# Attention-value products of two heads: float32 by turns on the two halves of the output columns, in place of three products of split halves on all columns

## The chip, the cores and the metric

The kernel runs on one core of a Trainium2 chip. Its metric is the device time of one execution in microseconds (us). The engines are TensorE (PE; its weight loads are listed as PEld), VectorE (DVE), ScalarE (ACT), GpSimd (POOL) and SyncE (SP, which issues the weight DMAs). PE products go to PSUM and are read from there by DVE or ACT.

## The reference

One sequence of 256 positions by 1024 features runs through three blocks: a layer of gated softmax attention with forget gates ("fox") and one of compressed, selected and windowed attention ("nsa"); a layer of stick-breaking and dilated attention with a feed-forward network; a layer of pooling and block attention with a mixture of experts. Every attention ends in the same kind of product: probabilities times values, per head of 64 columns.

```
p = jax.nn.softmax(logits, axis=-1).astype(v.dtype)          # fox, nsa, dilated, block attention
w = jnp.where(mask, jnp.exp(log_sigmoid(z) + after), 0.0)    # stick-breaking
o = jnp.einsum('bhqk,bkhd->bqhd', p, v)                      # the product that the change concerns
```

There are 16 heads in fox, 16 in nsa (each with two such products, selected and windowed, on top of a small one with compressed keys), 16 in the second block's mixer (8 stick-breaking, 8 dilated) and 8 in the third's. All is float32.

## The kernel before

Activations lie transposed, features on the 128 partitions, 256 positions along the free side. Weights come as pieces of 128x1024 by DMA. ACT rounds each piece to a high part (`whi`, line 241) and DVE makes the low part (`wlo`, line 242); a projection is three products per 128x128 tile (lines 450 to 452: high by high, low by high, high by low), in the type float32r. These projections are most of PE's instructions.

In each mixer a generator for the attention is woven between the steps of the projections (`weave`, with a rate for each mixer). What the generators record is not yet the order on an engine: a scheduler places each engine's instructions by when it reckons their operands to be ready, so an attention product can be parted by products of the projections. Per head the attention makes scores (lines 545, 546, 555 or 961, 962), a softmax, three transpositions on PE into a PSUM tile `t`, a copy of it into SBUF, and the product with the values. Keys are in two blocks of 128, and the first 128 queries see only the first, so the probabilities of a head are 384 columns: 256 for key block 0, 128 for key block 1.

The last two steps are done in two ways:

- fox and the second block's mixer ("mixer2"): ACT writes the rounded probabilities into `pth` (line 610) and DVE the rest into `ptl` (line 611), for a pair of heads side by side; the values are split likewise when they leave PSUM, `vh` by ACT (line 601) and `vl` by DVE (line 602). `pair_av` (line 628) then takes the values of both heads, 128 columns wide, as the weights, and streams both heads' probabilities: three products of 512 columns for key block 0 and three of 256 for key block 1. Half of what it writes is one head's probabilities by the other head's values, and is not read: `gated_pair` and `finish` take the two right quarters, in two instructions each (lines 646 and 1123).
- nsa and the third block's mixer ("mixer3"): `attn_transpose` copies the transposed probabilities in float32 to `ptw` (line 588, three buffers), and `attn_av` (lines 595 and 596) does one head at a time in float32, its 64 value columns as the weights, into the half of the output tile `o` that belongs to the head. Each float32 product appears in the trace as two weight loads and two matmuls. In nsa the four products of a chunk (two heads, two branches) follow one product of all 128 columns with 32 rows (`VCB`, line 1013).

Of the kernel before, what the change touches and what calls it, by code (L numbers as in the profile page):

```python
# [9 lines left out]
F32 = mybir.dt.float32  # L10
# [5 lines left out]
OP = mybir.AluOpType  # L16
# [254 lines left out]
def program(tc, A, out, upto=99):  # L271
    nc = tc.nc
    ctx = ExitStack()
    with ctx:
# [323 lines left out]
        def values(dst, c, p, r):  # L598
# [5 lines left out]
        def probs(pt, h, src):  # L604


            if h % 2 == 0:
                pt[h // 2] = [ph.tile([P, 2, 384], F32R, name=n, bufs=2) for n in ("pth", "ptl")]
# [4 lines left out]
        def transposed(pn):  # L613
            p = ps.tile([P, 384], F32, name="t")
            for i in range(3):
                nc.tensor.transpose(p[:, i * P:i * P + P], pn[:, i * P:i * P + P], ident)
            return p

        def pair_av(pt, v, c):


            o = ps.tile([P, 2, S], F32, name="o")
            hi, lo = pt
            for kb in range(2):
                q = slice(0, S) if kb == 0 else slice(S, S + P)
                vh, vl = (t[:, kb, c] for t in v)
                for i, (w, x) in enumerate(((vh, hi), (vl, hi), (vh, lo))):
                    nc.tensor.matmul(o[:, :, kb * P:], w, x[:, :, q], start=kb == 0 and i == 0, stop=kb == 1 and i == 2)
            return o

# [7 lines left out]
        def gated(og, c, po, sz):  # L638
            t = wk.tile([P, S], F32, name="sp")
            nc.vector.tensor_tensor(t, po, sz[:, c, :], op=OP.mult)  # L640
            split(og, c, t)

        def gated_pair(og, c, o, sz):
            t = wk.tile([P, S], F32, name="sp")
            for e, a in enumerate(HALF):
                nc.vector.tensor_tensor(t[a], o[a, e, :], sz[a, c, :], op=OP.mult)
            split(og, c, t)
# [32 lines left out]
        def fox(st1):  # L680
# [50 lines left out]

            vN = [ph.tile([P, 2, D], F32R, name=n) for n in ("vh", "vl")]
# [16 lines left out]
            def fox_attn():  # L749
                st, pt = {}, {}  # L750
# [35 lines left out]
        def nsa(st1):  # L786
# [159 lines left out]
            def attn():  # L946
# [48 lines left out]

                def trans(c):
                    for e in range(2):
                        for b in range(2):
                            stage[c, e, b] = attn_transpose(stage[c, e, b], CP[b])
                            yield  # L1000
                    p = ps.tile([32, 256], F32, name="t")
                    c2 = stage[c, "c"]
# [4 lines left out]
                    stage[c, "c"] = t  # L1007
                    yield

                def av(c):  # L1010
                    gp = c // 4
                    o = ps.tile([P, S], F32, name="o")
                    nc.tensor.matmul(o, VCB[:, gp, :], stage[c, "c"], start=True, stop=False)
                    for e in range(2):
                        oh = o[e * 64:e * 64 + 64, :]
                        g = 2 * gp + e
                        for b in range(2):
                            attn_av(oh, stage[c, e, b], lambda kb: vN[:, kb, b * 256 + g * 64:b * 256 + g * 64 + 64], False, b == 1)
                            yield
                    while cnt["z"] <= c:  # L1020
                        yield
                    gated(og, c, o, sz)
                    yield

                for i in range(9):
                    if i:
                        while len(done) < 2:
                            yield
                        yield from comp(i - 1)
                    if i < 8:  # L1030
                        while cnt.get("nq", 0) <= i:
                            yield
                        yield from scores(i)
                    if i:
                        yield from trans(i - 1)
                        yield from av(i - 1)

# [47 lines left out]
        def mixer2(st1):  # L1085
# [18 lines left out]

            vN = [ph.tile([P, 2, D], F32R, name=n) for n in ("vh", "vl")]

            def v_evac(c, tb, p):
                values(vN, (tb, slice(c * 512, c * 512 + 512)), p, rc[:, tb:tb + 1])

# [10 lines left out]
            def finish(c, po):  # L1120
                o = ph.tile([P, S], F32, name="fo", bufs=2)
                for e, a in enumerate(HALF):
                    nc.scalar.copy(o[a], po[a, e, :])
                sq = wk.tile([P, S], F32, name="sq")
                nc.scalar.activation(sq, o, AF.Square)
                p = ps.tile([P, S], F32, name="t")
# [8 lines left out]
            def attn():  # L1135
                st, pt = {}, {}

                for i in range(19):
# [24 lines left out]
                    if 1 <= i <= 16:  # L1163
                        h = i - 1
                        if h < 8:
                            z, sp = st[h]
                            nc.tensor.matmul(z[:, 0:384], C["ntri"], sp, start=False, stop=False, skip_group_check=True)
                            nc.tensor.matmul(z[:, 128:256], neg, sp[:, 256:384], start=False, stop=True, skip_group_check=True)
                            w = wk.tile([P, 384], F32, name="ptw")
                            nc.scalar.activation(w, z[:, 0:384], AF.Exp)  # L1170
                            probs(pt, h, w)
                        else:
                            probs(pt, h, transposed(st[h]))
                        yield
                    if i >= 3 and i % 2 == 1 and i <= 17:
                        c = (i - 3) // 2
                        finish(c, pair_av(pt.pop(c), vN, slice(c * P, c * P + P)))
                        yield
# [73 lines left out]
        def mixer3(st1):  # L1252
# [58 lines left out]
            def attn():  # L1311
                st, po = {}, {}
                for i in range(11):
# [11 lines left out]
                    if 2 <= i <= 9:  # L1325
                        h = i - 2
                        c = h // 2
                        if h % 2 == 0:
                            po[c] = ps.tile([P, S], F32, name="o")
                        attn_av(po[c][(h % 2) * 64:(h % 2) * 64 + 64, :], st[h], lambda kb: vN[:, kb, h * 64:h * 64 + 64])  # L1330
                        if h % 2 == 1:
                            nc.scalar.copy(oa[0][:, c, :], po[c])
                            nc.vector.tensor_tensor(oa[1][:, c, :], po[c], oa[0][:, c, :].bitcast(F32), op=OP.subtract)
                        yield
# [412 lines left out]
```

## Time and profile before

| | us |
|---|---|
| median of three runs | 1717.55 (1711.0 to 1719.35) |
| the profiled execution | 1714.88 |
| its span, first to last instruction | 1713.1 |
| PE busy | 1658.1 (97%) |
| PE weight loads busy | 1532.3 (89%) |
| DVE busy | 1304.1 (76%) |
| ACT busy | 976.3 (57%) |

A matmul's length in the trace is from its start to its modelled end, and the next one starts before that: what one costs the engine is read from start to start. The stages of the four mixers lie at about 28 to 160 us (fox), 200 to 345 (nsa, whose attention starts near 230), 360 to 490 (mixer2) and 720 to 800 (mixer3's attention). The mean granted TensorE clock is 0.994.

### The profile page before, as it was taken

How to read it: one execution, taken by the hardware profiler on the slowest of the kernel's cores; microseconds unless marked ns; L12 is line 12 of the kernel's file. 1: busy time of each engine (PE TensorE's matmuls, PEld its weight loads, DVE VectorE, ACT ScalarE, POOL GpSimd, SP SyncE). 2: the span in 40 equal slices, each digit the busy share in tenths (PEclk: the TensorE clock that was granted, in tenths of full speed). 3: DMA queues.
4: the chain of work that ended last, by engine and by line, in shares of the span. 5: the costliest groups of instructions: out<-in, count | busy, mean ns of one | idle time of the engine just before them, and what ended most of it. 6: DMA issues, size and time to landing. Idle time of an engine off the chain costs nothing.

```text
span 1713.1 us, 31723 instructions
## 1 busy us (share of the span) xinstructions
PE 1658.1 (97%) x12052; PEld 1532.3 (89%) x12052; DVE 1304.1 (76%) x2715; ACT 976.3 (57%) x1853; POOL 189.4 (11%) x198
## 2 busy tenths in 40 slices
PE   9999999989899999999999999999999999999997
PEld 7999888778789999889999999999999988888886
DVE  6887878699867766786768988888999566666665
ACT  5775567558855555566544455554444555555554
POOL 2000244340130000111046000000000000000000
PEclk9999999999999999999999999999999999999999
DMA  7444542387437877435555555454454556555663
GB/s 252 136 136 150 169 166 64 105 268 243 149 111 259 267 262 245 143 118 173 175 172 161 161 164 157 159 161 156 155 161 159 174 195 196 190 193 195 196 189 120
DMA packets 84088, 300.07 MB, mean 175 GB/s; under 512 B 10144, under 2 KB 11040, under 8 KB 83680
## 3 DMA queue, kind: packets, MB, share of 16 engines
q1 hardware_dynamic: 83360, 296.39, 53.5%
q8 instruction: 94, 1.54, 0.4%
q10 hardware_dynamic: 576, 1.66, 0.3%
q14 instruction: 58, 0.48, 0.1%
HBM read 296.04 MB, written 1.05 MB: 173 GB/s over the span
## 4 chain that ended last, share of the span: by engine, by line
PE 52%; DVE 3%; ACT 0%; issue 0%; POOLq 0%; POOL 0%; DVEq 0%; ACTq 0%
PE s L1624 10%; PE t L1624 10%; PE pj L450 5%; PE pj L451 5%; PE pj L452 5%; PE o L1584 3%; PE s L450 2%; PE t L450 2%; PE s L452 2%; PE s L451 2%; PE t L451 2%; PE t L452 2%; DVE wlo L242 1%; PE s L1433 0%; PE o L595 0%
## 5 line engine op out<-in xcount | busy, mean ns | idle before, releaser
L241 ACT CAST whi<-wraw 128x1024 fp32r<-128x1024 f32 x504 | 528.9, 1051 | 359.0 <-PE pj L451 108.7
L242 DVE TENSOR_TENSOR wlo<-wraw,whi 128x1024 fp32r<-128x1024 f32 x486 | 601.1, 1241 | 168.2 <-ACT whi L241 165.7
L450 PE MATMUL pj<-hxh,whi 128*128 128x256 f32 x1448 | 417.0, 288 | 7.0 <-DVE vl L602 4.5
L452 PE MATMUL pj<-hxh,wlo 128*128 128x256 f32 x1448 | 410.5, 284 | 1.2 <-DVE wlo L242 0.9
L451 PE MATMUL pj<-hxl,whi 128*128 128x256 f32 x1448 | 410.8, 284 | 0.6 <-DVE hxl L1193 0.3
L450 PEld LDWEIGHTS pj<-hxh,whi 128*128 128x128 f32 x1448 | 276.4, 191 | 11.6 <-DVE vl L602 5.4
L451 PEld LDWEIGHTS pj<-hxl,whi 128*128 128x128 f32 x1448 | 276.2, 191 | 2.7 <-DVE hxl L1193 1.0
L452 PEld LDWEIGHTS pj<-hxh,wlo 128*128 128x128 f32 x1448 | 276.0, 191 | 2.9 <-DVE wlo L242 1.7
L1624 PE MATMUL s<-whi,hxl 128*128 128x512 f32 x512 | 157.8, 389 | 0.0
L1624 PE MATMUL t<-whi,hxl 128*128 128x512 f32 x512 | 157.6, 389 | 0.0
L1612 ACT CAST hxl<-a 128x256 fp32r<-128x256 f32 x128 | 52.1, 408 | 152.0 <-PE t L1624 150.2
L450 PE MATMUL s<-hxh,whi 128*128 128x256 f32 x456 | 130.7, 287 | 1.7 <-DVE st L572 1.7
L452 PE MATMUL s<-hxh,wlo 128*128 128x256 f32 x456 | 129.0, 283 | 0.4 <-DVE wlo L242 0.4
L451 PE MATMUL s<-hxl,whi 128*128 128x256 f32 x456 | 128.9, 283 | 0.0
L450 PE MATMUL t<-hxh,whi 128*128 128x256 f32 x432 | 124.6, 288 | 1.3 <-ACT whi L241 1.3
L452 PE MATMUL t<-hxh,wlo 128*128 128x256 f32 x432 | 122.8, 284 | 1.7 <-DVE wlo L242 1.5
L451 PE MATMUL t<-hxl,whi 128*128 128x256 f32 x432 | 122.4, 283 | 0.0
L1624 PEld LDWEIGHTS t<-whi,hxl 128*128 128x128 f32 x512 | 96.1, 188 | 19.9
L1624 PEld LDWEIGHTS s<-whi,hxl 128*128 128x128 f32 x512 | 95.9, 188 | 20.0 <-ACT hxl L1612 0.2
L1613 DVE TENSOR_TENSOR hxl<-a,hxl 128x256 fp32r<-128x256 f32 x128 | 54.3, 425 | 62.6 <-PE t L1624 60.5
L291 DVE SCALAR_TENSOR_TENSOR wraw<-wraw,cb 128x1024 f32<-128x1024 f32 x48 | 59.6, 1241 | 44.5 <-DMA wraw<-in_ada 44.2
L450 PEld LDWEIGHTS s<-hxh,whi 128*128 128x128 f32 x456 | 87.0, 191 | 2.1 <-issue 1.9
(409 smaller groups left out, 3401.5 us busy)
## 6 DMA issues: line engine op xcount, KB each, us to landing
wraw<-in_pu SPq DMA_DIRECT2D x128, 512.0 KB
wraw<-in_pv SPq DMA_DIRECT2D x128, 512.0 KB
wraw<-in_b_ffn SPq DMA_DIRECT2D x66, 512.0 KB
wraw<-in_ada SPq DMA_DIRECT2D x48, 512.0 KB
wraw<-in_b_qk SPq DMA_DIRECT2D x24, 512.0 KB
wraw<-in_fox_qk SPq DMA_DIRECT2D x16, 512.0 KB
wraw<-in_b_o SPq DMA_DIRECT2D x16, 512.0 KB
wraw<-in_b_g SPq DMA_DIRECT2D x16, 512.0 KB
```

The costliest lines, as they stand in the source:

```text
L241: nc.scalar.copy(hi, r)
L242: (nc.gpsimd if self.np in self.on_pool else nc.vector).tensor_tensor(lo, r, hi.bitcast(F32), op=OP.subtract)
L291: nc.vector.scalar_tensor_tensor(t, t, 1.0, cb, op0=OP.mult, op1=OP.mult, accum_out=modT[:, i:i + 1])
L450: nc.tensor.matmul(o, wh, xh, start=start, stop=False)
L451: nc.tensor.matmul(o, wh, xl, start=False, stop=False)
L452: nc.tensor.matmul(o, wl, xh, start=False, stop=stop)
L1584: nc.tensor.matmul(p[:, t, :], x[:, w[0], :, w[1]], y[i][:, w[0], :, w[1]], start=i == 0 and t == 0, stop=i == 2, skip_group_check=True)
L1612: nc.scalar.copy(ah, src)
L1613: nc.vector.tensor_tensor(al, src, ah.bitcast(F32), op=OP.subtract)
L1624: nc.tensor.matmul(acc[tb][h], x[:, t], w[:, h * 512:h * 512 + 512], start=n == 0 and i == 0, stop=n == P - 1 and i == 2)
```

## The change

All four mixers now use one way: values in one float32 tile (`vN`), transposed probabilities in float32 (`ptw`), and an `attn_av` that takes a pair of heads and writes, for each key block, first the even head's product into partitions 0 to 63 of the output and then the odd head's into partitions 64 to 127. `values`, `probs`, `transposed`, `pair_av` and `gated_pair` are gone. In nsa the two branches of a chunk are now transposed and multiplied one after the other (`trans_av`), and the order of the copies between DVE and ACT goes by head instead of by branch.

```diff
-        def attn_av(o, pt, v, start=True, stop=True):
-            nc.tensor.matmul(o, v(0), pt[:, 0:256], start=start, stop=False)
-            nc.tensor.matmul(o[:, 128:256], v(1), pt[:, 256:384], start=False, stop=stop)
+        def attn_av(o, pts, v, start=True, stop=True):
+            for kb in range(2):
+                for e, a in enumerate(HALF):
+                    nc.tensor.matmul(o[a, kb * P:], v(e, kb), pts[e][:, kb * S:kb * P + S], start=start and not kb, stop=stop and kb == 1)
...
-            hi, lo = (t[:, c[0], c[1]] for t in dst)
-            nc.scalar.mul(hi, p, r)
-            nc.vector.scalar_tensor_tensor(lo, p, r, hi.bitcast(F32), op0=OP.mult, op1=OP.subtract)
...
-            hi, lo = (t[:, h % 2, :] for t in pt[h // 2])
-            nc.scalar.copy(hi, src)
-            nc.vector.tensor_tensor(lo, src, hi.bitcast(F32), op=OP.subtract)
...
             def v_evac(c, tb, p):
-                values(vN, (tb, slice(c * 512, c * 512 + 512)), p, rc[:, tb:tb + 1])
+                nc.scalar.mul(vN[:, tb, c * 512:c * 512 + 512], p, rc[:, tb:tb + 1])
...
                     if 1 <= i <= NH:
-                        probs(pt, i - 1, transposed(st[i - 1]))
+                        st[i - 1] = attn_transpose(st[i - 1])
...
-                        o = pair_av(pt.pop(c), vN, slice(c * P, c * P + P))
+                        o = ps.tile([P, S], F32, name="o")
+                        attn_av(o, [st.pop(2 * c + e) for e in range(2)], lambda e, kb: vN[:, kb, c * P + e * 64:c * P + e * 64 + 64])
...
-                        gated_pair(og, c, o, sz)
+                        gated(og, c, o, sz)
...
+                    for b in range(2):
+                        pts = []
+                        for e in range(2):
+                            pts.append(attn_transpose(stage.pop((c, e, b)), CP[e]))
                             yield
+                        if not b:
+                            o = ps.tile([P, S], F32, name="o")
+                            nc.tensor.matmul(o, VCB[:, gp, :], t, start=True, stop=False)
+                        attn_av(o, pts, lambda e, kb: vN[:, kb, b * 256 + gp * P + e * 64:b * 256 + gp * P + e * 64 + 64], False, b == 1)
+                        yield
...
-                for e, a in enumerate(HALF):
-                    nc.scalar.copy(o[a], po[a, e, :])
+                nc.scalar.copy(o, po)
...
                             nc.scalar.activation(w, z[:, 0:384], AF.Exp)
-                            probs(pt, h, w)
+                            st[h] = w
```

On PE, in fox, the product of the first pair of heads stands in the order of before so (`vh`, `vl` are the parts of the values, `pth`, `ptl` those of the probabilities, and the numbers count buffers):

```order
L452 MATMUL pj_732<-hxh_127,wlo_618 128x256
L628 MATMUL o_751<-pth_580,vh_157 128x512
L628 MATMUL o_751<-pth_580,vl_158 128x512
L628 MATMUL o_751<-ptl_581,vh_157 128x512
L628 MATMUL o_751<-pth_580,vh_157 128x2x128
L628 MATMUL o_751<-pth_580,vl_158 128x2x128
L628 MATMUL o_751<-ptl_581,vh_157 128x2x128
L450 MATMUL pj_732<-hxh_127,whi_617 128x256
```

and in the order of the changed kernel so (`ptw_575` and `ptw_661` are the two heads):

```order
L452 MATMUL pj_723<-hxh_127,wlo_611 128x256
L597 MATMUL o_742<-ptw_575,vN_157 64x256
L597 MATMUL o_742<-ptw_661,vN_157 64x256
L597 MATMUL o_742<-ptw_575,vN_157 64x128
L597 MATMUL o_742<-ptw_661,vN_157 64x128
L450 MATMUL pj_723<-hxh_127,whi_610 128x256
```

Six products of all output columns became four of one half each, the heads by turns, with products of the projection right ahead and behind as before.

On PE, in nsa, the fourth chunk before (`L1013` is the product with the compressed values; three of the chunk's four pieces follow it, the fourth stands a few rows further down by itself):

```order
L452 MATMUL pj_3601<-hxh_1776,wlo_3493 128x256
L1013 MATMUL o_3649<-ct_3647,VCB_2105 128x256
L595 MATMUL o_3649<-ptw_3618,vN_2104 64x256
L596 MATMUL o_3649<-ptw_3618,vN_2104 64x128
L595 MATMUL o_3649<-ptw_3624,vN_2104 64x256
L596 MATMUL o_3649<-ptw_3624,vN_2104 64x128
L595 MATMUL o_3649<-ptw_3630,vN_2104 64x256
L596 MATMUL o_3649<-ptw_3630,vN_2104 64x128
L974 MATMUL t_3669<-KC_2101,qk_2529 128x32 x2
```

and the same chunk's first branch in the changed kernel (`L975` is the product with the compressed values; `L584` to `L586` transpose the next branch, `L924` and `L925` are scores):

```order
L975 MATMUL o_3586<-ct_3572,VCB_2060 128x256
L597 MATMUL o_3586<-ptw_3578,vN_2059 64x256
L584 MATMUL t_3598<-ident_90,pn_3281 128x128
L585 MATMUL t_3598<-ident_90,pn_3281 128x128
L586 MATMUL t_3598<-ident_90,pn_3281 128x128
L452 MATMUL pj_3802<-hxh_1731,wlo_3558 128x256
L597 MATMUL o_3586<-ptw_3584,vN_2059 64x256
L597 MATMUL o_3586<-ptw_3578,vN_2059 64x128
L924 MATMUL s_3496<-k2_2473,q2_3487 128x256
L925 MATMUL s_3496<-kl_2474,q2_3487 128x256
```

The pieces of one branch, which the code writes as four in a row, are parted here by products of all columns, and the last of them (`ptw_3584`, 64x128) follows after four more scores.

## Rows read from the trace of the kernel before

**Rows 1.** The page, part 1: busy us, share of span, instruction count of each engine.

```profile
PE 1658.1 (97%) x12052; PEld 1532.3 (89%) x12052; DVE 1304.1 (76%) x2715; ACT 976.3 (57%) x1853; POOL 189.4 (11%) x198
```

**Rows 2.** Stretches: us, then busy PE, PEld, DVE, ACT, POOL, granted clock, DMA, GB/s.

```profile
28.00:150.00 122.00, 118.28 (x908) 112.82 (x907) 106.10 (x255) 86.03 (x192) 7.45 (x10) 1.00 0.44 138
200.00:340.00 140.00, 131.17 (x976) 115.34 (x975) 106.53 (x346) 88.29 (x230) 55.90 (x78) 0.98 0.35 114
380.00:480.00 100.00, 93.14 (x665) 83.48 (x666) 82.41 (x173) 82.15 (x195) 9.03 (x18) 1.00 0.55 183
```

**Rows 3.** Timeline of PE in fox: start us, length us, line, out<-in, shape, count.

```profile
60.55 0.39 PE L628 MATMUL o<-pth,vh 128*128 128x512 f32 x1
...
61.58 0.28 PE L450 MATMUL pj<-hxh,whi 128*128 128x256 f32 x1
```

**Rows 4.** Timeline of PE in mixer3, around one head's product.

```profile
782.61 0.28 PE L452 MATMUL pj<-hxh,wlo 128*128 128x256 f32 x1
782.82 0.65 PE L595 MATMUL o<-ptw,vN 128*64 128x256 f32 x2
...
783.61 0.39 PE L450 MATMUL pj<-hxh,whi 128*128 128x256 f32 x1
783.84 0.28 PE L451 MATMUL pj<-hxl,whi 128*128 128x256 f32 x1
783.96 0.28 PE L452 MATMUL pj<-hxh,wlo 128*128 128x256 f32 x1
```

**Rows 5.** Timeline of PE in nsa, the first chunk's four head products.

```profile
239.25 0.65 PE L595 MATMUL o<-ptw,vN 128*64 128x256 f32 x2
239.73 0.38 PE L596 MATMUL o<-ptw,vN 128*64 128x128 f32 x2
239.95 0.65 PE L595 MATMUL o<-ptw,vN 128*64 128x256 f32 x4
240.38 0.44 PE L596 MATMUL o<-ptw,vN 128*64 128x128 f32 x4
240.68 0.65 PE L595 MATMUL o<-ptw,vN 128*64 128x256 f32 x2
...
241.47 0.63 PE L974 MATMUL t<-KC,qk 128*128 128x32 f32 x4
241.94 0.36 PE L450 MATMUL pj<-hxh,whi 128*128 128x256 f32 x1
```

**Rows 6.** Waits of PE from 28 to 150 us: us in total, times, longest.

```profile
PE s L545 <- ACT stc L535: 1.2, 2, 0.9
PE pj L450 <- DVE vl L602: 1.1, 1, 1.1
```

**Rows 7.** Waits of PE from 376 to 480 us.

```profile
PE pj L450 <- DVE vl L602: 3.4, 1, 3.4
...
PE s L545 <- ACT ptw L1170: 1.0, 2, 0.5
```

**Rows 8.** Timeline of all engines, mixer2's first product after the values.

```profile
378.29 1.26 ACT L601 ACTIVATE vh<-pj,rcol 128x512 fp32r<-128x512 f32 x2
...
379.56 1.40 DVE L602 SCALAR_TENSOR_TENSOR vl<-pj,rcol,vh 128x512 fp32r<-128x512 f32 x2
...
380.35 0.39 PE L450 MATMUL pj<-hxh,whi 128*128 128x256 f32 x1 [3.42 <-DVE vl L602]
```

**Rows 9.** Groups by line and shape: count, busy us, mean ns, idle before.

```profile
L242 DVE TENSOR_TENSOR wlo<-wraw,whi 128x1024 fp32r<-128x1024 f32 x486 | 601.1, 1241 | 168.2 <-ACT whi L241 165.7 <-PE o L628 0.4
L588 DVE COPY ptw<-t 128x384 f32<-128x384 f32 x24 | 13.1, 546 | 0.7 <-PE t L586 0.5
L610 ACT CAST pth<-t 128x384 fp32r<-128x384 f32 x24 | 11.3, 469 | 4.0 <-PE t L616 4.0
```

**Rows 10.** Two stretches around nsa's last chunk, columns as in rows 2.

```profile
327.00:331.00 4.00, 2.97 (x17) 1.81 (x17) 2.42 (x11) 0.74 (x2) 0.76 (x2) 0.98 0.00 0
331.00:335.00 4.00, 4.00 (x19) 2.79 (x18) 0.32 (x1) 0.48 (x1) 0.29 (x2) 0.59 0.00 0
```

More of the change, by code (lines that the diff above doesn't have):

```diff
@@ L591, in program @@
         CP = (nc.vector.tensor_copy, nc.scalar.copy)
-        def attn_av(o, pt, v, start=True, stop=True):
-            nc.tensor.matmul(o, v(0), pt[:, 0:256], start=start, stop=False)
-            nc.tensor.matmul(o[:, 128:256], v(1), pt[:, 256:384], start=False, stop=stop)
-        def values(dst, c, p, r):
-            hi, lo = (t[:, c[0], c[1]] for t in dst)
-            nc.scalar.mul(hi, p, r)
-            nc.vector.scalar_tensor_tensor(lo, p, r, hi.bitcast(F32), op0=OP.mult, op1=OP.subtract)
-        def probs(pt, h, src):
-            if h % 2 == 0:
-                pt[h // 2] = [ph.tile([P, 2, 384], F32R, name=n, bufs=2) for n in ("pth", "ptl")]
-            hi, lo = (t[:, h % 2, :] for t in pt[h // 2])
-            nc.scalar.copy(hi, src)
-            nc.vector.tensor_tensor(lo, src, hi.bitcast(F32), op=OP.subtract)
[L613 to L623, printed above, removed]
-            for kb in range(2):
[L625 to L629, printed above, removed]
+        def attn_av(o, pts, v, start=True, stop=True):
+            for kb in range(2):
+                for e, a in enumerate(HALF):
+                    nc.tensor.matmul(o[a, kb * P:], v(e, kb), pts[e][:, kb * S:kb * P + S], start=start and not kb, stop=stop and kb == 1)
         def resid(nxt):
@@ L730, in f_evac @@
                         r = r2
-            vN = [ph.tile([P, 2, D], F32R, name=n) for n in ("vh", "vl")]
+            vN = ph.tile([P, 2, D], F32, name="vN")
             def v_evac(c, tb, p):
@@ L994, in comp, with trans_av @@
                     yield
[L996 to L1000, printed above, removed]
+                def trans_av(c):
+                    gp = c // 4
                     p = ps.tile([32, 256], F32, name="t")
-                    c2 = stage[c, "c"]
+                    c2 = stage.pop((c, "c"))
                     for qb in range(2):
@@ L1006, in trans @@
                     nc.vector.tensor_copy(t, p)
-                    stage[c, "c"] = t
                     yield
[L1010 to L1018, printed above, removed]
-                            yield
+                    for b in range(2):
+                        pts = []
+                        for e in range(2):
+                            pts.append(attn_transpose(stage.pop((c, e, b)), CP[e]))
+                            yield
+                        if not b:
[3 more added lines that the diff above has]
+                        yield
                     while cnt["z"] <= c:
@@ L1034, in attn @@
                     if i:
-                        yield from trans(i - 1)
-                        yield from av(i - 1)
+                        yield from trans_av(i - 1)
             drain(proj(4, hx, c_evac, banks=("s", "t")))
@@ L1103, in mixer2 @@
                 nc.gpsimd.tensor_scalar(xT[:, kt, :], xT[:, kt, :], V["gf"][:, kt:kt + 1], ALPHA, op0=OP.mult, op1=OP.mult)
-            vN = [ph.tile([P, 2, D], F32R, name=n) for n in ("vh", "vl")]
+            vN = ph.tile([P, 2, D], F32, name="vN")
             def v_evac(c, tb, p):
-                values(vN, (tb, slice(c * 512, c * 512 + 512)), p, rc[:, tb:tb + 1])
+                nc.scalar.mul(vN[:, tb, c * 512:c * 512 + 512], p, rc[:, tb:tb + 1])
             def qk_evac(c0, p, m):
@@ L1121, in finish @@
                 o = ph.tile([P, S], F32, name="fo", bufs=2)
-                for e, a in enumerate(HALF):
-                    nc.scalar.copy(o[a], po[a, e, :])
+                nc.scalar.copy(o, po)
                 sq = wk.tile([P, S], F32, name="sq")
-                nc.scalar.activation(sq, o, AF.Square)
+                nc.scalar.activation(sq, po, AF.Square)
                 p = ps.tile([P, S], F32, name="t")
@@ L1170, in attn @@
                             nc.scalar.activation(w, z[:, 0:384], AF.Exp)
-                            probs(pt, h, w)
+                            st[h] = w
                         else:
-                            probs(pt, h, transposed(st[h]))
+                            st[h] = attn_transpose(st[h])
                         yield
@@ L1176, in attn @@
                         c = (i - 3) // 2
-                        finish(c, pair_av(pt.pop(c), vN, slice(c * P, c * P + P)))
+                        o = ps.tile([P, S], F32, name="o")
+                        attn_av(o, [st.pop(2 * c + e) for e in range(2)], lambda e, kb: vN[:, kb, c * P + e * 64:c * P + e * 64 + 64])
+                        finish(c, o)
                         yield
@@ L1324, in attn @@
                         yield
[L1325 to L1333, printed above, removed]
+                    if i >= 3 and i % 2 == 1 and i <= 9:
+                        c = (i - 3) // 2
+                        o = ps.tile([P, S], F32, name="o")
+                        attn_av(o, [st.pop(2 * c + e) for e in range(2)], lambda e, kb: vN[:, kb, c * P + e * 64:c * P + e * 64 + 64])
+                        nc.scalar.copy(oa[0][:, c, :], o)
+                        nc.vector.tensor_tensor(oa[1][:, c, :], o, oa[0][:, c, :].bitcast(F32), op=OP.subtract)
                         yield
```

10 lines of the change are left out of this document (3 added, 7 removed).

## The prediction

> **What bounds the kernel now.** I read the share of busy time first, then the busy times by stretch, then PE's timeline around each kind of attention product, and last who PE waits for. PE is busy for 97% of the span [rows 1], and the change lies in the attention of four mixers, some 400 us of 1713, where PE is busy too: 118 of 122 us in fox, 131 of 140 in nsa, 93 of 100 in mixer2 [rows 2]. So what counts is how long PE's new products take from the last product before them to the first at full pace behind, and then which of PE's few waits go. DVE and ACT are no bound over the whole, but in mixer2 both are busy for 82 of 100 us [rows 2].
>
> **The change part by part.**
>
> *A pair today, in fox and mixer2.* The six products of one pair run from 60.55 to 61.58, 1.03 us, and the projection goes on at once [rows 3]: they use all columns, as their neighbours do. Eight pairs in each stage are 8.24 us.
>
> *A head by itself in float32, on half the columns.* In mixer3 the last full-width product starts at 782.61, the head's product at 782.82, the next full-width one at 783.61 and the one behind it at 783.84 [rows 4]. From 782.61 to 783.84 are 1.23 us. Two full-width products take 0.12 each at their usual pace (783.84 to 783.96), so the head costs 1.00. Its own streaming is less: key block 0 takes 0.43 (239.95 to 240.38) and key block 1 0.22 (239.73 to 239.95) [rows 5], together 0.65. The other 0.35 is the price of going from full width to half width and back: about 0.1 idle on the way in, 0.05 on the first pass (two take 0.48 at 239.25), 0.1 idle on the way out, and a first product behind that takes 0.23 instead of 0.12 [rows 4, 5]. It is paid once for each run of half-width products, however long.
>
> *Two heads on different halves run side by side.* One head's four passes go from 239.25 to 239.95, 0.70 us. From 239.95 to 240.68, 0.73 us, two heads' eight passes are done: the first line of that stretch counts four passes of 256 where a head alone has two, and they start together [rows 5]. So a pair on different halves costs what one head does, plus 0.03: 1.03 us with the change of width. That is what the six products cost today. In fox and mixer2 a whole pair gains and loses nothing.
>
> TensorE's page in the Trainium skill (TensorE: Matmul & The Clock Gate, "The mechanism" in the part on packing small matmuls) says that matmuls start and end strictly in program order, only weight loads being drawn ahead. The trace disagrees: in the program the first head's second branch stands as a whole ahead of the second head's product, and yet their first passes start together at 239.95. I go by the trace; the page's order is a rival below.
>
> *How often the width changes.* In the changed order the half-width products stand in 54 runs, against 22 before (counted over the whole order). Of 36 pairs, 20 stand whole; 16 are parted, mostly as one product of key block 0, other products, and the remaining three. A lone product of key block 0 costs 0.35 + 0.43 = 0.78, a lone one of key block 1 0.57, a run of three 1.03 (its longer half has both key blocks), a run of two 0.78.
> - Fox: six whole pairs, one as 3 + 1, one as 1 + 3: 6.18 + 1.60 + 1.81 = 9.59, against 8.24: +1.35.
> - Mixer2: five whole, one whole with the next pair's first product behind it (1.46), that pair's other three (1.03), and one as 1 + 3 (1.81): 9.45, +1.2.
> - Mixer3: before, six heads whole and two parted (0.78 + 0.57): 8.7. Now three pairs as 1 + 3 and one as 1 + 2 + 1: 5.43 + 2.13 = 7.56, -1.1.
> - Nsa: before, four chunks in one run, 239.25 to 241.47 and 0.13 of change, 2.35 each; four with the last quarter by itself, 1.62 + 1.00: 19.8 in all. Now eight whole (8.24), six as 1 + 3 (10.86), two as 1 + 2 + 1 (4.26): 23.4. Three of the eight products with the compressed values no longer stand ahead of a half-width one, +0.2 each for a change of their own; and 13 runs are followed by small products, which don't show the slow first one (four passes in 0.47, 241.47 to 241.94 [rows 5]), -0.1 each. Sum 22.7, +2.9.
>
> PE's products together: +4.4 us.
>
> *The values.* In fox and mixer2 the eight subtractions `vl` go. Twice they hold PE, because a projection tile needs the PSUM bank: 1.1 us in fox, 3.4 in mixer2 [rows 6, 7]. In mixer2 PE goes on at 380.35, after the first `vl` (from 379.56); the first of ACT's two multiplications, 378.29 to about 378.92, would free it at some 379.0 [rows 8]. ACT is late next, so 1.35 of 3.4 goes. In fox I take the whole 1.1. Bounds: 0 (ACT as late as DVE) and -4.5. Taken: -2.45.
>
> *The probabilities.* ACT's cast (0.47) goes for 32 heads. DVE's subtraction goes for the same 32, and a copy of the same tile (0.55) comes for 24 of them; the stick-breaking eight need none [rows 9]. So ACT has 15 us less, and DVE what eight subtractions take. Mostly this lies under PE's projections. What it may lift are PE's waits for ACT: 1.2 us for `stc` in fox, 1.0 for `ptw` in mixer2 [rows 6, 7], between 0 and -2.2; taken -1.5. At the ends of fox and mixer2, where projections to fill with run out, the chain from the last transposition to the product is shorter by one cast: 0.47 each, -1.0. The output's two evictions that become one, on DVE in fox and on ACT in mixer2, I cost at nothing, since projections are on PE meanwhile; at the last pair uncovered they would give a few tenths.
>
> *Nsa's copies.* Before, a chunk transposed all its pieces and then multiplied. Now each branch is transposed, copied and multiplied in turn. In the last two chunks, where there is little else for PE, the second head's copy (0.55) has 0 to 0.5 us of PE's work ahead of its use: some 0.4 us late at four places, +1.5. The last chunk is the one in which the clock already fell, to 0.59 from 331 to 335 us, after PE had been busy for 2.97 of the 4 us before [rows 10]; I leave that as it is. Queued behind a waiting product are the next projections, and behind them the freeing of weight pieces.
>
> *Sum.* +4.4 - 2.45 - 1.5 - 1.0 + 1.5 = +0.95 us. The profiled execution took 1714.88 (its span, 1713.1, and 1.8 around it) and lies between the runs' lowest, 1711.0, and their median, 1717.55. The middle of all four is 1716.2; with the sum, 1717.
>
> **The rivals.** No change is within 0.5%, 8.6 us: from 1709 to 1726.
>
> *A. The relief of ACT and DVE is worth more (faster).* PE is idle for 3.7 us in fox and 6.9 in mixer2's stretch, and 3 more wait for `vl` just ahead of that [rows 2, 7]. If all of it goes, 13.6 us: 1716.2 + 4.4 + 1.5 - 13.6 = 1708.5. For it: DVE and ACT near 82% in mixer2. Against it: PE's waits there are also for POOL, which has as much to do as before.
>
> *B. The products wait for copies in nsa (slower).* In 12 of the 16 branches only 0.1 to 0.6 us of other work for PE stands between the second head's transpositions and the product of its copy. The copy takes 0.55 and can stand behind a weight piece's subtraction of 1.24 on DVE [rows 9], up to 1.2 us late. It decides from 0.65 us on the average: 12 such waits are 8 us. At 0.9 each: 1717 + 11 = 1728. For it: DVE is busy for 107 of nsa's 140 us [rows 2]. Against it: the scheduler parted the pairs just where it reckoned the second copy late.
>
> *C. The two heads don't run side by side (the change doesn't do what it says).* Then each of the 20 whole pairs takes 0.62 more (1.30 + 0.35 for 1.03), and the shorter runs 3.7 together: 1717 + 16 = 1733. Rows 5 speak against it.
>
> *D. Starts in strict order.* The odd head's first pass could then start only with the even head's second, and the pair takes five slots, 3 x 0.215 + 2 x 0.11 = 0.87, in place of 0.65: +0.2 for 20 pairs, 1721, no change. This is the page's order from above.
>
> **How the numbers follow.** The forecast has 0.59, A 0.17, B 0.12, C 0.05, D 0.07. Of A some 0.13 is faster than 1709, and 0.03 of the forecast, whose own range is 1709 to 1725: faster 0.16. Slower is most of B, all of C and 0.02 of the forecast: 0.17. The rest, 0.67, is no change. The range of 8 in 10 reaches into A and to B's price: 1705 to 1730.
>
> **What would show it.** In the trace after: 288 passes of the new line in 54 runs, a whole pair's first passes of both halves starting within about 0.05 us of each other, and 1.0 to 1.05 us from full pace to full pace. If the second half starts 0.2 us later, it is D; if only after the first half's four passes, C. The wait of `pj` for `vl` is gone, and in mixer2 PE goes on at ACT's first multiplication. PE's waits for `ptw` in nsa below 3 us bear out the forecast, 8 us or more B. PE idle in mixer2's stretch of under 3 us would be A. The forecast is wrong if the time leaves 1709 to 1725, or if it stays there by two large terms that cancel.

## The result and the profile after

The changed kernel takes 1700.93 us (median of 4 runs, 1699.54 to 1702.84), beside 1716.61 for the kernel before: a ratio of 0.9911, 95% interval 0.9895 to 0.9927. It is 12 to 18 us faster; the forecast of 1717, no change, was wrong.

The page of the changed kernel, part 1 (busy us, share of the span, instructions), answers to [rows 1]:

```profile
PE 1655.5 (97%) x12084; PEld 1522.2 (90%) x12084; DVE 1295.2 (76%) x2691; ACT 963.5 (57%) x1813; POOL 182.8 (11%) x198
```

PE is busy for 2.6 us less in a span that is 13.9 shorter (1699.2). So most of the gain is idle time of PE that is gone (time at the low clock counts as busy here). To see where, I took stretches that hold the same work in both. Each runs from a stage's first projection product to the first product of the part behind it: in fox the first of the norm, in nsa the first of mixer2's values, in mixer2 the first of the norm ahead of the feed-forward. They are fox, nsa, mixer2 and the feed-forward behind it; columns as in [rows 2]. Before:

```profile
37.31:161.66 124.35, 121.72 (x969) 117.92 (x970) 106.85 (x255) 87.35 (x197) 7.45 (x10) 1.00 0.45 141
202.22:351.98 149.76, 141.45 (x1072) 126.24 (x1073) 116.42 (x363) 97.10 (x243) 55.90 (x78) 0.98 0.38 126
380.35:493.53 113.18, 105.71 (x768) 95.53 (x768) 93.39 (x184) 88.91 (x202) 15.75 (x24) 1.00 0.56 186
493.53:701.60 208.07, 202.29 (x1633) 197.60 (x1633) 147.57 (x223) 110.31 (x175) 5.52 (x8) 1.00 0.72 236
```

After:

```profile
36.27:159.80 123.53, 122.18 (x985) 115.33 (x986) 102.66 (x244) 82.80 (x182) 7.42 (x10) 1.00 0.43 143
200.64:346.20 145.56, 140.70 (x1072) 121.78 (x1073) 118.69 (x363) 98.95 (x243) 53.32 (x78) 1.00 0.39 129
372.78:482.35 109.57, 104.95 (x784) 94.16 (x785) 90.58 (x175) 79.91 (x178) 16.42 (x24) 0.98 0.60 197
482.35:688.55 206.20, 201.84 (x1635) 197.15 (x1633) 147.95 (x224) 110.72 (x175) 5.54 (x8) 1.00 0.72 239
```

PE's idle time (length less busy time) falls from 2.6 to 1.4 us in fox, 8.3 to 4.9 in nsa, 7.5 to 4.6 in mixer2. Nsa is 4.2 shorter and mixer2 3.6. The clock column matters too: 0.98 stands in nsa before, and in mixer2 after.

**The products did what was forecast.** The timeline of PE in mixer2 after, around a whole pair (start us, length us, line, out<-in, shape, count), to be set beside [rows 3, 4]:

```profile
397.19 0.28 PE L452 MATMUL pj<-hxh,wlo 128*128 128x256 f32 x1
397.40 0.87 PE L597 MATMUL o<-ptw,vN 128*64 128x256 f32 x8
398.20 0.39 PE L450 MATMUL pj<-hxh,whi 128*128 128x256 f32 x1
398.42 0.28 PE L451 MATMUL pj<-hxl,whi 128*128 128x256 f32 x1
```

From 397.19 to 398.42 are 1.23 us, less two products at full pace (0.12 each): the pair costs about 1.00. In the whole kernel 54 runs of half-width products stand, with 288 passes. Summed over these runs, fox went from 9.1 to 9.65 us, mixer2 from 9.45 to 9.25, mixer3 from 8.8 to 7.7, nsa from 21.6 to 25.0: +2.6 in all.

**Waits went.** PE's waits in nsa before, 202 to 352 us (us, times, longest), largest first:

```profile
PE t L584 <- POOL pn L578: 1.9, 3, 1.4
PE s L450 <- DVE st L572: 1.7, 1, 1.7
PE t L1004 <- DVE cm L992: 1.7, 2, 1.2
PE t L886 <- DVE ch L882: 1.1, 1, 1.1
PE t L584 <- DVE ptw L588: 0.5, 1, 0.5
```

and after, 200.5 to 346.2:

```profile
PE s L924 <- DVE st L565: 1.2, 2, 0.9
PE t L849 <- DVE ch L845: 1.1, 1, 1.1
PE o L597 <- DVE ptw L588: 0.8, 2, 0.5
PE pj L451 <- DVE hxl L355: 0.7, 1, 0.7
```

With the smaller ones these lists add up to 8.6 and 5.0 us. The copies of the transposed probabilities, as ACT makes them in nsa, show one reason; the row before (count, busy us, mean ns, idle before, by releaser), then the row after:

```profile
L588 ACT COPY ptw<-t 128x384 f32<-128x384 f32 x16 | 7.6, 474 | 10.5 <-PE o L596 9.4 <-PE t L586 0.9
```

```profile
L588 ACT COPY ptw<-t 128x384 f32<-128x384 f32 x16 | 7.5, 471 | 9.3 <-PE t L586 9.2
```

Before, a chunk had four copies alive and three buffers: ACT waited 9.4 us for PE's last product of the piece whose buffer it needed, and the transposed piece in PSUM had to stay until its copy was made. After, a branch needs two buffers, and ACT, which waits nearly as long, waits only for its source. How this reached PE is not shown by these rows, since only 0.5 us of PE's list is a wait for such a copy; that it counts is tested by e6 below.

In mixer2, from its first projection product to its end, PE's largest waits before are these, beside the one for `vl` and the 1.0 for `ptw` of [rows 7]:

```profile
PE t L616 <- POOL pn L578: 3.2, 3, 1.4
PE s L545 <- ACT stc L535: 0.7, 1, 0.7
PE o L420 <- POOL acc L415: 0.5, 1, 0.5
```

and after, beside the values' wait (2.3):

```profile
PE t L584 <- POOL pn L578: 1.4, 3, 0.6
PE s L545 <- ACT ptw L1126: 1.3, 3, 0.6
PE t L585 <- POOL pn L578: 1.0, 1, 1.0
```

With the smaller ones, and without the values' wait, these add up to 6.5 and 4.4 us.

**And the clock.** Before, two gaps of PE in nsa were followed by a fall of TensorE's clock from 2.4 to 1.2 GHz; [rows 10] show one, this is the other:

```profile
241.00:245.00 4.00, 3.90 (x30) 3.26 (x28) 1.79 (x6) 1.33 (x3) 2.73 (x4) 1.00 0.79 256
245.00:249.00 4.00, 1.96 (x13) 1.57 (x14) 3.19 (x9) 0.65 (x3) 2.83 (x3) 0.99 0.29 52
249.00:253.00 4.00, 4.00 (x19) 3.33 (x18) 1.78 (x3) 1.04 (x1) 0.00 (x0) 0.58 0.26 100
```

PE was busy for 1.96 of 4 us; then the clock is at 0.58, and 19 products are counted in 4 us, where 35 are at full clock (328 to 332 below). That is 0.42 x 4 = 1.7 us lost, behind the wait itself. After, the tail of nsa keeps its clock, and one fall stands at mixer2's start:

```profile
324.00:328.00 4.00, 3.41 (x25) 2.21 (x26) 1.25 (x3) 0.96 (x2) 0.99 (x2) 1.00 0.00 0
328.00:332.00 4.00, 4.00 (x35) 3.74 (x32) 2.19 (x6) 1.40 (x4) 1.93 (x5) 1.00 0.55 184
370.00:374.00 4.00, 1.68 (x13) 1.25 (x12) 2.14 (x4) 2.22 (x3) 4.00 (x5) 1.00 0.85 315
374.00:378.00 4.00, 4.00 (x24) 4.00 (x23) 3.06 (x5) 1.04 (x1) 0.96 (x1) 0.57 0.91 293
```

Not every gap is followed by a fall. Before, at the same place, PE was busy for 0.93 us in 4, and the clock stayed:

```profile
376.00:380.00 4.00, 0.93 (x5) 0.43 (x3) 2.42 (x4) 2.21 (x3) 4.00 (x5) 1.00 0.92 334
380.00:384.00 4.00, 3.65 (x30) 3.65 (x31) 4.00 (x6) 1.79 (x2) 0.43 (x1) 1.00 0.77 257
```

### The profile page after: what moved, and what is told of

Its sections match the earlier page's. It is cut to its first block, busy times and chain, and to the rows that moved or that the text cites. A ratio compares the mean times of both kernels' runs of the same rounds, so it can differ in the third digit from the quotient of the medians.

```text
span 1699.2 us, 31714 instructions
## 1 busy us (share of the span) xinstructions
PE 1655.5 (97%) x12084; PEld 1522.2 (90%) x12084; DVE 1295.2 (76%) x2691; ACT 963.5 (57%) x1813; POOL 182.8 (11%) x198
## 4 chain that ended last, share of the span: by engine, by line
PE 53%; DVE 3%; ACT 1%; issue 0%; POOL 0%; POOLq 0%; DVEq 0%; ACTq 0%
PE s L1579 10%; PE t L1579 10%; PE pj L450 5%; PE pj L451 5%; PE pj L452 5%; PE o L1539 3%; PE s L450 2%; PE t L450 2%; PE s L452 2%; PE s L451 2%; PE t L451 2%; PE t L452 2%; DVE wlo L242 1%; PE s L1388 0%; PE o L597 0%
## 5 line engine op out<-in xcount | busy, mean ns | idle before, releaser
L452 PEld LDWEIGHTS s<-hxh,wlo 128*128 128x128 f32 x456 | 87.0, 191 | 0.9 <-DVE wlo L242 0.8
```

What stands on the lines that cost most here:

```text
L452: nc.tensor.matmul(o, wl, xh, start=False, stop=stop)
```

## The experiments

All times are medians, with the ratio to the kernel before beside which they ran and its 95% interval. This table gives stage lengths from each profile, in us, worked out from the starts of PE's products, with what was lost at the low clock inside the stage in brackets (half its time there). "Values" is the time from the last product of the values to the next projection product. "Fox" here goes on through its output projection, to the first product of nsa's values, where "ahead of nsa" starts; "mixer3 to end" goes from the end of mixer3's values to PE's last product. Mixer2's weights (24.6 before, 23.9 after) and the stretch between the feed-forward and mixer3 are not in the table.

| kernel | values, fox | fox | ahead of nsa | nsa | values, mixer2 | mixer2 | feed-forward | mixer3 to end |
|---|---|---|---|---|---|---|---|---|
| before | 1.48 | 148.4 | 16.5 (1.7) | 149.8 (3.4) | 3.8 | 113.2 | 208.1 | 979.4 |
| e14 | 1.48 | 148.2 | 17.9 (3.4) | 148.4 (1.7) | 4.1 | 115.2 (1.7) | 209.4 | 980.0 |
| e6 | 1.48 | 148.2 | 18.2 (3.4) | 146.0 (1.7) | 5.8 (1.5) | 113.7 (1.9) | 211.9 (1.7) | 980.4 |
| e2 | 1.48 | 148.5 | 16.6 (1.7) | 145.4 | 5.3 (0.6) | 114.1 (2.8) | 206.5 | 979.3 |
| e1 | 0.48 | 147.5 | 14.3 | 149.9 (3.4) | 3.6 (0.3) | 111.0 (3.1) | 208.5 | 979.4 |
| after | 0.48 | 147.6 | 16.8 (1.7) | 145.6 | 2.7 | 109.6 (1.7) | 206.2 | 978.5 |
| after, again | 0.48 | 147.6 | 14.9 | 145.2 | 3.0 | 112.1 (3.4) | 205.2 | 978.6 |
| e4 | 1.48 | 147.5 | 14.6 | 145.4 | 3.7 | 110.2 (3.4) | 208.2 | 978.5 |
| e10 | 0.48 | 147.6 | 14.3 | 145.6 | 2.9 | 111.1 (1.7) | 204.6 | 978.6 |
| e3 | 0.48 | 146.6 | 16.5 (1.7) | 150.9 (1.7) | 2.7 | 110.6 (1.7) | 206.4 | 978.6 |
| e13 | 1.48 | 147.8 | 14.7 | 146.0 | 5.1 (0.5) | 114.2 (2.9) | 205.0 | 978.6 |
| e5 | 0.48 | 147.8 | 14.4 | 148.8 (3.4) | 2.5 | 110.5 (1.7) | 208.3 | 979.8 |
| x1 | 0.48 | 147.2 | 14.3 | 141.7 | 3.0 | 110.5 | 207.3 | 978.6 |

**e1, the change in fox and mixer2 alone** (from the changed kernel, nsa and mixer3 put back).

```diff
-                        yield from trans_av(i - 1)
+                        yield from trans(i - 1)
+                        yield from av(i - 1)
```

> The kernel before with the change in fox and mixer2 alone (nsa and mixer3 as before). Theory S (the gain is a sum of stages, each from its own waits): fox gives about -1.9 us, mixer2 -4.7 from the values' wait and fewer waits for transpositions and scores, and some -1.9 follow in the feed-forward behind mixer2, so about 1708 against 1716.6, nsa's length as before within 1 us. Rival N (the gain is nsa's, by its order and by the clock that no longer falls there; fox and mixer2 only seemed shorter): 1715 to 1717. Rival P (the products themselves are cheaper than reckoned): whole pairs below 0.9 us from full pace to full pace.

Measured: 1705.35, ratio 0.9935 (0.9915 to 0.9955), 8 to 15 us faster by itself. Fox and mixer2 are shorter, nsa is as before, with its two falls of the clock. The 1708 of S lies inside the interval. N and P are refuted: whole pairs cost 1.00.

**e2, the change in nsa alone.** The reverse edit on the kernel before.

> The kernel before with the change in nsa alone. Theory S: nsa is 4.2 us shorter (149.8 to about 145.6 from its first projection product to the next weights' first), fox, mixer2 and the feed-forward behind it keep their lengths within 0.5, time about 1712.5 against 1716.6. Rival N: the time is that of the whole change, 1701 to 1704, with mixer2 shorter too although its code is as before. If the feed-forward behind mixer2 is 1.9 shorter here too, its part of the gain does not come from mixer2.

Measured: 1711.43, ratio 0.9976 (0.9962 to 0.9989). Nsa is 4.4 shorter, with no fall of the clock in it; of that 3.4 is the clock. The two parts, 11.5 (e1) and 5.4, add up to 16.9, the whole within the intervals. The feed-forward is 206.5 here with mixer2 as before, and 208.5 in e1 with mixer2 as changed: its 1.9 don't come from mixer2's change. Mixer2 did not keep its length within 0.5: free of the clock it has 111.3 here and 113.2 before, with the same code. So a difference of 2 us in this stage, between two profiles, is not yet one of the code.

**e3, the probabilities by way of ACT and DVE again.**

```diff
+            hi = ph.tile([P, 384], F32R, name="pth", bufs=2)
+            nc.scalar.copy(hi, src)
+            pt = wk.tile([P, 384], F32, name="ptw")
+            nc.vector.scalar_tensor_tensor(pt, hi.bitcast(F32), 0.0, src, op0=OP.mult, op1=OP.add)
```

> The changed kernel with the probabilities of fox and mixer2 once more by way of a cast on ACT and a combination of cast and source on DVE, as long as the subtraction of before (384 columns each, 32 heads); products in float32 as changed. Theory R (the relief of ACT and DVE at the probabilities is what shortens mixer2 and fox): mixer2 is some 3 us longer than in the changed kernel, fox some 1, time 1704 to 1706 against 1701. Rival V (only the values' subtraction and the shape of the products count): 1700 to 1702, mixer2 within 0.7.

Measured: 1704.8, ratio 0.9938 (0.992 to 0.9957). The time is R's, but the stages aren't: mixer2 is 1.1 longer, fox 1.0 shorter, and the difference to the changed kernel is in nsa, where no code differs: there PE waited once for a weight piece, and the clock fell behind it. The two waits, from 198 to 349 us:

```profile
PE pj L450 <- ACT whi L241: 2.8, 1, 2.8
...
PE pj L452 <- DVE wlo L242: 0.8, 1, 0.8
```

The piece was late because ACT, which rounds it, had been held by the issue of one DMA of its own (`cb`):

```profile
327.43 5.70 ACTq L296 DMA_DIRECT2D cb<-in_c  x1
333.18 0.51 ACT L370 ACTIVATE hxh<-xT,vecs 128x256 fp32r<-128x256 f32 x1 [5.86 <-PE t L452]
```

The changed kernel has this for the same issue, and the other profiles have 0.38 there too:

```profile
329.33 0.38 ACTq L296 DMA_DIRECT2D cb<-in_c  x1
```

So in this profile the stages of the edit give the probabilities' relief no worth (+1.1 - 1.0), and nsa's 5.4 (the two waits and 1.7 of the clock) go back to this late issue, which no other profile has. But the median is 3.9 us longer than the changed kernel's, and five of the six runs (1702.78 to 1708.42) lie above all of its eight (1696.97 to 1702.84). Whether the late issue stood in the other five, which have no profile, is not known, so what the probabilities are worth in the time stays open.

**e5, head after head in place of by turns.**

```diff
-            for kb in range(2):
-                for e, a in enumerate(HALF):
+            for e, a in enumerate(HALF):
+                for kb in range(2):
```

> The changed kernel with the products of a pair head after head (both key blocks of the even head, then both of the odd one) in place of by turns, in all four mixers. Theory I (the two column halves take their work independently, as in nsa before, where the second head's passes began beside the first head's second branch): the odd head's first pass still starts within 0.05 us of the even head's, a pair costs 1.0 us as by turns, time 1700 to 1703. Rival T (the turns matter): the odd head starts 0.4 to 0.65 us later, each of 20 whole pairs costs 0.4 to 0.6 more and the parted ones about as much in all, time 1712 to 1723.

Measured: 1706.21, ratio 0.9944 (0.9926 to 0.9963); below T's 1712, above I's 1703. The timeline around a whole pair in mixer2:

```profile
399.60 0.28 PE L452 MATMUL pj<-hxh,wlo 128*128 128x256 f32 x1
399.81 0.88 PE L597 MATMUL o<-ptw,vN 128*64 128x256 f32 x8
400.62 0.39 PE L450 MATMUL pj<-hxh,whi 128*128 128x256 f32 x1
400.84 0.28 PE L451 MATMUL pj<-hxl,whi 128*128 128x256 f32 x1
```

1.24 us against 1.23 by turns: the two heads run side by side in either order, the odd one's first pass 14 ns behind the even one's. In the program both products of the even head stand ahead of the odd head's, and yet the even head's second product starts 0.47 us behind the odd head's first. T is refuted for the pair. The order of the scheduler differs around parted pairs (55.7 us for all products against 51.6), and in this profile nsa had two falls of the clock (3.4); either is of the size to make much of the 5 us, and no run takes them apart.

**e4, the values' subtraction back** (its result unused).

```diff
+                lo = ph.tile([P, 512], F32R, name="vl", bufs=2)
+                nc.vector.scalar_tensor_tensor(lo, p, rc[:, tb:tb + 1], vN[:, tb, c * 512:c * 512 + 512], op0=OP.mult, op1=OP.subtract)
```

> The changed kernel with the values' subtraction back: the eight DVE operations of 512 columns in fox and mixer2 that read the same PSUM tile, their result unused. Theory W (the subtraction holds PSUM banks from the projections): fox's first projection product starts 1.4 to 1.5 us after the values' last again in place of 0.48, mixer2's 3.8 in place of 2.7; the stages behind that keep their lengths within 0.7; time 1702 to 1704 against 1701. Rival M (the subtractions are also what delays mixer2's first heads): mixer2 itself is 2 us or more longer, time 1704 to 1707.

Measured: 1703.5, ratio 0.9921 (0.9893 to 0.9949). Both waits came back, 1.00 in fox and 1.00 in mixer2; mixer2 itself, free of the clock, has 106.8 against 107.9, so it isn't longer for it: W against M. That it is 1.1 shorter with more work on DVE is scatter, and outside the 0.7 that W allowed.

**e6, a fourth buffer in nsa before** (to make room, another tile of nsa, `ce`, has one buffer in place of two).

```diff
-            pt = wk.tile([P, 384], F32, name="ptw")
+            pt = wk.tile([P, 384], F32, name="ptw") if own is None else own.tile([P, 384], F32, name="ptx", bufs=1)
```

> The kernel before with a fourth buffer in nsa for the copies of the transposed probabilities (a chunk has four of them alive at once, the pool has three). Theory B (nsa's gain is that a branch holds only two copies, so that transpositions no longer wait for a buffer): nsa goes from 154.4 to 150 to 152 us up to the next weights' last product, with fewer low-clock stretches in it, time 1712 to 1714. Rival O (the order of the products, not the buffers, made nsa shorter): nsa stays at 153 to 155, time 1715 to 1718.

Measured: 1714.88, ratio 0.9985 (0.9972 to 0.9997). Nsa is 3.8 shorter, 1.7 of it the clock's: B for the stage, and 2.6 us (0.5 to 4.8) in the time, about half of what the whole change in nsa gives (e2). The profiled run was the slowest of ten (1721.16), with falls of the clock in later stages.

**e10, mixer2's output in two halves again, the square from the copy.**

```diff
-                nc.scalar.copy(o, po)
+                for a in HALF:
+                    nc.scalar.copy(o[a], po[a])
-                nc.scalar.activation(sq, po, AF.Square)
+                nc.scalar.activation(sq, o, AF.Square)
```

> The changed kernel with mixer2's output once more evicted in two halves by ACT, and the square taken from the evicted copy in place of PSUM, as before. Theory F (this chain holds PE at the product behind the square, 8 times): mixer2 is 1.5 to 2.5 us longer than in the changed kernel, PE waits for the square 1 us or more in all, time 1702 to 1704. Rival H (it is hidden, as the prediction had it at nothing): mixer2 within 0.5, time 1700 to 1702.

Measured: 1701.66, ratio 0.9915 (0.9889 to 0.994). Mixer2 is 1.5 longer than in the first profile of the changed kernel at the same clock, but free of the clock only 0.8 longer than in the second (109.4 against 108.7), and PE's named wait for the square is 0.7. F and H stay undecided, and the time alone can't tell.

**e13, all of ACT's and DVE's work in fox and mixer2 back** (e3, e4, e10 and fox's gate in halves together).

> The changed kernel with all work of ACT and DVE given back in fox and mixer2 (values' subtraction, probabilities' cast and subtraction, output in halves, square from the copy); only the products are in float32 by turns, and nsa and mixer3 as changed. Theory R (relief of ACT and DVE in small waits that add up): mixer2 is 4 to 5 us longer than in the changed kernel (its length free of low-clock stretches 107.9), fox with its values 1.5 to 2.5, time 1706 to 1709. Rival Q (the shape of the products and where the scheduler puts them is what counts): mixer2 1 to 2 longer, from the values and the square alone, time 1702 to 1704.

Measured: 1708.48, ratio 0.9953 (0.9939 to 0.9967): R's time, 7.6 us above the changed kernel, and its nine runs (from 1705.87) all lie above the changed kernel's eight. Without what the clock took, mixer2 has 113.2 before, 111.3 here, 107.9 after: 3.4 longer, between Q and R. Fox with its values is 1.2 longer, most of it the values' 1.00, below R's 1.5. This is more than the parts by themselves (in mixer2 e10 +0.8 to +1.5, e3 +1.1, e4 -1.1): with all of it back the copies are late, pairs are parted and waited for (13 runs for 14.7 us, against 9 for 9.25).

One profile of each is not enough for the tenths. Free of the clock, mixer2 with the products of before has 113.2, 113.5 (e14), 111.8 (e6) and 111.3 (e2), on the average 112.4; as changed it has 107.9, 108.7 (again) and 107.9 (e1), on the average 108.2. The 111.3 of e13 is 3.2 above that and within the range of before: the relief of ACT and DVE accounts for most of the 4.3, and what is left, 1.1, is no more than profiles of one code differ by.

**e14, the kernel before with the square taken straight from PSUM.**

```diff
+                    nc.scalar.activation(sq[a], po[a, e, :], AF.Square)
```

> The kernel before with mixer2's squares taken straight from PSUM, in two halves, ahead of the two copies (the changed kernel takes one square from PSUM behind one copy). Theory F (PE waits at the product behind the square for ACT's chain of two copies and a square): mixer2 is 0.7 to 1.5 us shorter (113.2 to about 112), time 1715 to 1716. Rival H (the chain is covered): mixer2 within 0.4 of before, time as before, 1716 to 1717.

Measured: 1717.91, ratio 1.0012 (1.0004 to 1.0021). Mixer2, free of the clock, 113.5: H. The square's chain was no bound in the order of before; what e10 shows, if it holds, belongs to the order of the changed kernel.

**x1, nsa's chunk as one run of sixteen passes by turns**, with a fourth buffer (and one in place of two for `ce`, as in e6), on the changed kernel.

```diff
+                    for b in range(2):
+                        for e in range(2):
+                            pts[b, e] = attn_transpose(stage.pop((c, e, b)), CP[e], ph if b and e else None)
...
+                    for b in range(2):
+                        attn_av(o, [pts[b, e] for e in range(2)], lambda e, kb: vN[:, kb, b * 256 + gp * P + e * 64:b * 256 + gp * P + e * 64 + 64], False, b == 1)
```

> The changed kernel with nsa's chunk once more as a whole: all four pieces transposed first (a fourth buffer for their copies), then the product with the compressed values and both branches' pairs by turns in one run of sixteen passes. Theory B (what nsa lost before was the third buffer, and what it loses now is the width changed 26 times): nsa's products fall from 25.0 us to 8 x 1.65 to 1.8 = 13 to 15, and the waits for buffers stay away, so nsa goes from 149.4 to 140 to 145, time 1692 to 1697. Rival O (branch by branch is what made nsa short, since a chunk's run waits for its last copy): the products fall, but PE waits as much more for copies and transpositions, nsa 148 to 152, time 1699 to 1704.

Measured: 1699.61, ratio 0.9908 (0.9894 to 0.9923), as the changed kernel beside it (1699.67). Its products in nsa cost 13.7 us in place of 25.0, and nsa:

```profile
197.42:339.12 141.70, 133.00 (x1072) 119.60 (x1073) 115.38 (x362) 96.73 (x243) 53.86 (x78) 1.00 0.39 134
```

PE is busy for 7.7 us less and idle for 8.7 in place of 4.9, on waits such as these:

```profile
PE t L584 <- DVE cst L950: 1.8, 1, 1.8
PE t L584 <- DVE cm L939: 1.5, 1, 1.5
PE t L584 <- POOL pn L578: 1.5, 2, 1.3
```

The 3.8 that remain are given back behind (mixer2's weights +1.6 against the first profile, mixer2 itself +1.9 to +2.7 against both, free of the clock). Both theories hold in part for the stage, O for the time.

**The changed kernel again.**

> The changed kernel once more, for its spread and a second profile beside the others. Stages that the change does not touch show by how much they move by themselves (the feed-forward behind mixer2 took 208.1 us before and 206.2 after; eight kernels so far have it between 204.6 and 211.9). Theory K (nsa has no low-clock stretch in the changed order): none between nsa's first projection and its end, nsa 149 to 150. Rival L (the first profile was lucky there): one or two such stretches, nsa 151 to 154. Time 1700 to 1703.

Measured: 1699.67, ratio 0.9903 (0.9888 to 0.9918). No fall of the clock in nsa: K. The stages that nothing touches moved by up to 2 us.

## Why the prediction was wrong

By the runs, it failed in two places of about the same size. For fox and mixer2 the terms of the sum come to -2.4 us (+1.35 +1.2 -2.45 -1.5 -1.0), and e1 measures -11.5. For nsa they come to +4.4 (+2.9 +1.5), and e2 measures -5.4.

- **Products, forecast +4.4: right in kind.** The pair costs 1.00 (forecast 1.03), two heads run side by side, 54 runs; +2.6 measured. Rivals C and D are out, and e5 shows that the turns aren't even needed for it. The page TensorE: Matmul & The Clock Gate of the Trainium skill says in "The mechanism" that matmuls start and end in program order. The trace of e5 disagrees with it: a product that stands two places later starts 14 ns behind the first, and ahead of the one between them.
- **Values, forecast -2.45: right.** 1.00 in fox and 1.1 in mixer2, given back by e4.
- **Probabilities, forecast -1.5 and -1.0 at the tails: open.** The stages of e3 give them no worth alone, its time 3.9 us that its one profile does not place.
- **Nsa, forecast +2.9 and +1.5: the first step that failed.** I added the price of more width changes, and late copies, to a stage in which PE was idle for 8.3 of 150 us [rows 2 has 8.8 of 140], as if PE were its bound throughout. Waits for `ptw` are 0.8 us, below the 3 forecast (rival B is out). What I left out is that the branches need two buffers in place of four, and that PE waits less: 8.6 us of named waits became 5.0. That the buffers count is shown by e6; that the rest of e2's 5.4 is the order of transposing and multiplying is argued, not tested by itself. x1 shows from the other side that PE's products are not the stage's bound throughout: 11.3 us of products less in nsa, and no gain in time.
- **"I leave that as it is", of the clock: the second step that failed.** The row that I quoted [rows 10] held the price. Nsa as before had one or two falls of the clock in four profiles of four (before, e1, e14, and e6 with its buffer); in the changed order none in six of seven (all but e3, behind its late DMA issue; e5 and x1 stand in other orders). This is 3.4 of the 4.2 us in nsa; but a fall of 1.7 stands in mixer2 after, so that over the two profiles the clock makes 1.7 of 13.9. Over all runs with a clock on record its mean was 0.9938 before (52 runs) and 0.9965 after (8): what is missing to 1, times the spans, is 10.6 and 5.9 us. By this estimate the clock makes at most 4.7 of the 15 us (less where PE had no work), and some 10 are something else.
- **Mixer2's relief at about nothing: the third step that failed.** Without the values, the sum's terms for mixer2 come to about 0 (products +1.2, less its part of the probabilities' -1.5, less a tail of 0.5), and the output stood at nothing. Free of the clock the stage is 5.3 shorter in the first profile, 4.3 on the average; 3.2 to 3.4 is ACT's and DVE's relief taken together (e13), of which no part by itself is clear. That is the mechanism of rival A, in mixer2, though its sign was not reached: PE is still idle for 5.0 us in 100 there (6.9 before). The rest I can't assign; in the profile 0.7 of it stands ahead of the mean's product at the stage's end, which started 0.83 after its neighbour before and 0.12 after. In e13 it is 0.12 too, so this part does not come from the relief.
- **Mixer3, forecast -1.1: right** (979.4 to 978.5).

The sum over the two profiles: values -2.1, fox -0.8, nsa -4.2, mixer2 -3.6 with the clock's 1.7 inside, its weights -0.7, the feed-forward -1.9, mixer3 -0.9, ahead of nsa +0.3: -13.9, as the spans have it. The feed-forward's part is not the change's by e1 and e2; it scatters from 204.6 to 211.9. The stretch ahead of nsa may hold another part: with fox as before it had falls of the clock in four profiles of four, with fox as changed in two of nine. The reason was not tested.

## What to carry to other kernels

Where an engine that is busy for 94% of a stage still waits, more or less work on it changes little until the waits are counted: x1 and this change both show it. On PE, price a wait with the low clock that may follow it, 1.7 us here, and look for it in the granted clock of the stretch behind. Before pricing a new order, count the buffers that are alive in it. And before a stage of one profile is put down to an edit, look at that stage in other profiles of the same code: here they differed by up to 2 us free of the clock, and in e3 by 5.4 after one late DMA issue.

## What was not expected of the hardware

The two column halves ran two heads' products side by side with the second head standing behind both products of the first (14 ns apart, e5). A granted clock of 0.57 to 0.59 came behind stretches of 4 us in which PE was busy for 1.68, 1.96 and 2.97 us [rows 10 has the last], but not behind one of 0.93. And once, in e3, the issue of one DMA held ACT for 5.70 us in place of 0.38; why is not known.
